# Layer 0's feed-forward by seven products over both halves of the sequence, in a two-layer block on one Trainium2 core

## The chip, the core and the metric

The kernel runs on one core of one Trainium2 chip. Its engines are TensorE (PE in the profile; PEld is its weight load), VectorE (DVE), ScalarE (ACT), GpSimd (POOL) and SyncE (SP), which issues most transfers. The metric is the device time of one execution in microseconds (us), as the median of several runs. A profile comes from one execution more; its span is what lies between the first and the last instruction.

## The reference

Two layers act on x of 1024 tokens by 1024 features, in 32-bit floats. A layer is

```python
h = rms_norm(x, g_pre_mix)
p = h @ w_in
a_pool, r_q, r_k, r_v, r_g, s_u, s_v, d_qkv, d_z, d_b, d_a = jnp.split(p, IN_SPLITS, axis=-1)
y = jnp.concatenate([pool_mixer(...), retention_mixer(...), spatial_gating_mixer(...), deltanet_mixer(...)], axis=-1)
x = x + rms_norm(y @ w_out, g_post_mix)
h = rms_norm(x, g_pre_ffn)
a, b = jnp.split(h @ w_up, 2, axis=-1)              # 2 x 2816 columns
a = causal_dwconv(a, conv_w) + conv_b               # three taps along the tokens
x = x + rms_norm((gelu(a) * b) @ w_down, g_post_ffn)
```

The four mixers are a windowed mean, a retention in chunks of 128 tokens, a gated spatial mixing, and a gated delta rule in chunks of 64 with a triangular solve per chunk. Retention, delta rule and both convolutions carry state along the tokens, so a half of the sequence needs the half before it.

## The kernel before

**Halves and precision.** The sequence is worked in two halves of 512 tokens. "Mixers (l,h)" means layer l, half h. A 32-bit operand is split into a rounded part (hi, on ScalarE) and the remainder (lo, on VectorE), and a product is three TensorE matmuls: hi·hi, hi·lo, lo·hi.

**The stages.** `win(l,h)` makes the input products (`a_unit`: one weight tile of 128 columns against 512 tokens, 24 matmuls; `b_units`: token blocks against 256 or 264 columns) and runs the mixers. `out(l,h)` is the output projection with the two norms behind it; `to_hT` transposes the normalized rows (L369) and splits them. `early(0,1)` makes some input products of mixers (0,1) in advance. `ffn(l,h)` is the plain feed-forward: for each of 22 tiles f of 128 features, two `a_unit`s, the convolution and gate, and, for every group of two f's, the down products (L1297 to L1299) into four accumulators.

**Layer 0** runs, in this order, mixers (0,0), mixers (0,1), `ffn(0,0)`, `out(0,1)`, `win(1,0)`, `ffn(0,1)`, `out(1,0)`. The feed-forward of a half gives TensorE work while the mixers of the next half take their many short dependent steps.

**Layer 1** has another form. Inside `win(1,1)` the argument `mid` starts `plain_part(1, ...)`, a generator: it does the first NPRE = 10 f's for half 0 the plain way, two at a time, with their down products (L1054 to L1056) into an accumulator that goes to DRAM (`accD`), and yields after each group of two. `run` lets it go on by NMIX = 2 groups before `out(1,1,mid)`, then closes the left part of the on-chip memory and opens pools for operand rows (`build`), then drains the generator, opens `pA0` and `pv` on the right, and makes the rest of the up products by seven products in place of eight: the normalized rows of a half, read back from DRAM (`hnD`, written by POOL at L326), are combined by four POOL additions (L1103 to L1106), transposed (L1112) and split into seven operands per half. `up_f` does the same with a tile pair of weights (four additions at L1159, seven splits at L1154 and L1155), multiplies (L1139, 84 matmuls 256 wide per half), and undoes the combination on the way out of PSUM. Its gate output goes to DRAM (`gD`) by a POOL transfer (L1213). Ten f's do so for half 1 alone (half 0 had them plainly), twelve for both halves. `down_full` then makes the down products of both halves.

**The order.** Program order gives each instruction its priority. A planner with its own costs then places the instructions of each engine one after another: at each moment the one of highest priority that it thinks ready, so that later work fills the holes it sees. `high_priority(offset=...)` moves evictions and weight casts ahead. What the planner fixes is a static order per engine and per transfer queue; on the chip an engine waits at an instruction that isn't ready, with all that stands behind it. A pool opened in the place of a closed one waits, tile by tile, for the last reader of the memory under it. `QUICK` lists the mixers whose steps are interleaved over two or three blocks of 128 tokens (`turns`); the others do one block at a time.

```python
QUICK = ((0, 0), (1, 1))
FULL = (1,)
NPRE, NMIX = 10, 2
```

`ORD1` is the order of the mixers' steps where a half other than (0,0) is in `QUICK`; its `x` calls `mid`. `FULL` lists the layers whose normalized rows are kept in `hnD`.

Of the kernel before, what the change touches and what calls it, by code (L numbers as in the profile page):

```python
# [10 lines left out]
F32R = mybir.dt.float32r  # L11
# [8 lines left out]
P = 128  # L20
# [16 lines left out]
QUICK = ((0, 0), (1, 1))  # L37
# [19 lines left out]
FULL = (1,)  # L57
NPRE, NMIX = 10, 2
# [60 lines left out]
class Net:  # L119
# [1023 lines left out]
    def up_f(self, l, f, halves, ahead=2000):  # L1143
# [14 lines left out]
        def add(o, a):  # L1158
            V.tensor_tensor(o, o, a, ALU.add)  # L1159

        with self.tc.high_priority(offset=ahead):
# [5 lines left out]
            add(b12, b22)  # L1167
# [4 lines left out]
            add(b21, b22)  # L1172
# [40 lines left out]
        nc.gpsimd.dma_start(self.gD[l][f, :, halves[0] * HALF:halves[0] * HALF + 2 * N], c)  # L1213

# [67 lines left out]
    def ffn(self, l, h, hT, mid=None):  # L1282
        self.up = UF
        nc, t, pf, st = self.nc, self.t, self.pf[l], self.state[l]
        V = nc.vector
        acc = self.acc_tiles()
        cf = st["cf"]
        def down(g0, gs):
            us = [self.unit(t["wD"][l, f], big=i == 3) for i, f in enumerate(g0)]
            for b in range(NB):  # L1290
                tb = slice(b * P, b * P + P)
                for n in range(2):
                    s = slice(n * 512, n * 512 + 512)
                    ps = self.ps()
                    for i, f in enumerate(g0):
# [3 lines left out]
                        nc.tensor.matmul(ps, lo[:, tb], us[i][0][:, s], start=False, stop=i == len(g0) - 1)  # L1299
                    with self.tc.high_priority(offset=1500):  # L1300
                        if g0[0] == 0:
# [3 lines left out]
        prev = None  # L1305
        tail = NF - GRP if l == DEPTH - 1 and h == 1 else NF
        groups = [list(range(f, min(f + GRP, NF))) for f in range(0, NF, GRP)]
        for fs in groups:
            f0 = fs[0]
            gs = []  # L1310
            for i, f in enumerate(fs):
                if i % 2 == 0:
                    cc = self.r4("c")
                pa = self.a_unit(t["wU"][l, 2 * f], hT)
                pb = self.a_unit(t["wU"][l, 2 * f + 1], hT)
                w = lambda j: pf[:, PF_CW + 3 * f + j:PF_CW + 3 * f + j + 1]
                cb = pf[:, PF_CB + f:PF_CB + f + 1]
                with self.tc.high_priority(offset=1500):
                    c = cc[:, i % 2 * HALF:i % 2 * HALF + HALF]
                    nc.scalar.activation(c, pa, AF.Identity, bias=cb, scale=w(2))  # L1320
                    if h == 0:
                        nc.scalar.copy(cf[:, f, :], pa[:, 510:512])
# [159 lines left out]
```

## Time and profile before

| what | value |
|---|---|
| time, median of 3 runs | 2557.81 us (2556.66 to 2564.56) |
| the profiled execution | 2557.59 us |
| its span | 2555.8 us |
| mean granted clock of TensorE | 0.978 |
| TensorE busy | 2435.4 us (95%) |
| VectorE busy | 1809.1 us (71%) |
| ScalarE busy | 983.0 us (38%) |
| GpSimd busy | 272.0 us (11%) |
| instructions | 38925 |

The lines of a profile are read like this. A group (`L215 PE MATMUL psg<-hT,whi 128*128 128x512 f32 x1312 | 523.4, 399 | ...`) names the line of the kernel, the engine, the operation, the tile written and the tiles read, the size and the count; behind the bar stand the busy time in us and the mean of one in ns, then the idle time of the engine just before, with what ended it. Matmuls overlap, so the mean of one is longer than the distance of two. A wait (`PE psg L1112 <- DMA hn<-hnD: 34.9, 4, 29.5`) names who waited, for whom, the sum in us, the count and the longest. In a table by stage, a stretch of the span stands first, then its length, the busy time of each engine with its count of instructions, the granted clock (1.00 is full speed), the mean busy share of the transfer engines and GB/s. All times count from the start of the span.

### The profile page before, as it was taken

What the parts mean: (1) busy time and instruction counts of PE and PEld (TensorE: products, weight loads), DVE (VectorE), ACT (ScalarE), POOL (GpSimd) and SP (SyncE); (2) the same over time, 40 slices, a digit from 0 to 9 for tenths busy, and PEclk for the clock granted to TensorE, in tenths of its full rate; (3) what the DMA queues carried; (4) which work ended last, traced back from release to release, by engine and by line L of the source; (5) the groups of instructions that cost most, each with busy time, mean ns of one, the idle gap of its engine ahead of it and who ended that gap; (6) DMA issues with size and microseconds to landing.
All of it is one profiled execution on the core that took longest, in us unless ns stands there. A gap on an engine that the chain in (4) does not pass through costs nothing.

```text
span 2555.8 us, 38925 instructions
## 1 busy us (share of the span) xinstructions
PE 2435.4 (95%) x15220; PEld 2093.1 (82%) x15220; DVE 1809.1 (71%) x3719; ACT 983.0 (38%) x1538; POOL 272.0 (11%) x389
## 2 busy tenths in 40 slices
PE   8989998999999999999999999999949799999998
PEld 7968987877788987787788898777838699999887
DVE  7895799765655898955665689976655777774747
ACT  5333452423332553332332355234432444443412
POOL 2321113000000013100000002211020200000000
PEclk9999998999999999999999999999969899999999
DMA  5233442322223552322222354222442332222723
GB/s 182 71 89 109 131 142 82 98 76 83 79 91 124 165 163 71 91 82 76 83 91 91 128 186 149 85 84 64 165 155 78 114 101 98 96 88 80 257 67 132
DMA packets 100221, 281.00 MB, mean 110 GB/s; under 512 B 30834, under 2 KB 31154, under 8 KB 99524
## 3 DMA queue, kind: packets, MB, share of 16 engines
q1 hardware_dynamic: 91428, 248.54, 30.7%
q0 software_dynamic: 8608, 29.96, 3.4%
q8 instruction: 120, 1.97, 0.3%
q14 instruction: 65, 0.53, 0.1%
HBM read 241.20 MB, written 37.26 MB: 109 GB/s over the span
## 4 chain that ended last, share of the span: by engine, by line
PE 75%; DVE 14%; DMA 4%; issue 4%; ACT 2%; POOL 1%; SPq 0%; DVEq 0%; ACTq 0%; POOLq 0%
PE psg L215 9%; PE psg L216 9%; PE psg L214 9%; PE psg L1139 7%; PE psm L1139 4%; PE psg L1297 3%; PE psg L1298 3%; PE psg L1299 3%; DVE pr L841 3%; PE psg L235 3%; PE psg L236 3%; PE psg L237 3%; DVE wlo L205 2%; PE psh L1139 2%; DVE A L843 1%
## 5 line engine op out<-in xcount | busy, mean ns | idle before, releaser
L216 PE MATMUL psg<-hT,wlo 128*128 128x512 f32 x1312 | 524.1, 401 | 0.0
L215 PE MATMUL psg<-hT,whi 128*128 128x512 f32 x1312 | 523.4, 399 | 0.2 <-DVE hT L373 0.2
L204 ACT CAST whi<-raw 128x1024 fp32r<-128x1024 f32 (+1 forms) x290 | 301.9, 1048 | 570.6 <-PE psg L215 229.0
L214 PE MATMUL psg<-hT,whi 128*128 128x512 f32 x1312 | 518.9, 396 | 0.1
L205 DVE TENSOR_TENSOR wlo<-raw,whi 128x1024 fp32r<-128x1024 f32 (+1 forms) x267 | 329.2, 1239 | 171.5 <-ACT whi L204 166.7
L214 PEld LDWEIGHTS psg<-hT,whi 128*128 128x128 f32 x1312 | 250.4, 191 | 56.5 <-ACT tmp L436 0.5
L215 PEld LDWEIGHTS psg<-hT,whi 128*128 128x128 f32 x1312 | 247.8, 189 | 57.9 <-DVE hT L373 0.8
L216 PEld LDWEIGHTS psg<-hT,wlo 128*128 128x128 f32 x1312 | 247.5, 189 | 53.7 <-issue 0.4
L1304 DVE TENSOR_TENSOR acc<-acc,psg 128x512 f32<-128x512 f32 x160 | 109.1, 686 | 72.7 <-PE psg L1299 72.1
L236 PE MATMUL psg<-wlo,hT 128*128 128x256 f32 (+1 forms) x512 | 149.9, 294 | 7.2 <-DVE wlo L205 5.7
L235 PE MATMUL psg<-whi,hT 128*128 128x256 f32 (+1 forms) x512 | 147.1, 291 | 3.2 <-ACT tmp L436 1.9
L237 PE MATMUL psg<-whi,hT 128*128 128x256 f32 (+1 forms) x512 | 149.2, 292 | 0.0
L235 PE MATMUL psg<-whi,y 128*128 128x256 f32 x512 | 142.8, 285 | 5.8 <-ACT whi L204 3.1
L1154 ACT CAST w<-wraw 128x512 fp32r<-128x512 f32 x154 | 91.4, 620 | 143.5 <-PE psg L1139 74.9
L236 PE MATMUL psg<-wlo,y 128*128 128x256 f32 x512 | 143.6, 283 | 0.8 <-DVE rv L297 0.8
L237 PE MATMUL psg<-whi,y 128*128 128x256 f32 x512 | 143.7, 284 | 0.0
L1297 PE MATMUL psg<-whi,g 128*128 128x512 f32 x352 | 140.2, 400 | 0.0
L1298 PE MATMUL psg<-wlo,g 128*128 128x512 f32 x352 | 138.8, 394 | 0.0
L1299 PE MATMUL psg<-whi,g 128*128 128x512 f32 x352 | 138.0, 392 | 0.0
L1155 DVE TENSOR_TENSOR w<-wraw,w 128x512 fp32r<-128x512 f32 x154 | 103.2, 695 | 37.4 <-ACT w L1154 37.1
L841 DVE SCALAR_TENSOR_TENSOR pr<-A 64x1 f32<-64x1 f32 (+30 forms) x124 | 110.2, 889 | 9.8 <-POOL A L837 7.5
L236 PEld LDWEIGHTS psg<-wlo,hT 128*128 128x128 f32 x512 | 99.5, 194 | 11.3 <-DVE wlo L205 6.4
(472 smaller groups left out, 5158.9 us busy)
## 6 DMA issues: line engine op xcount, KB each, us to landing
raw<-in_wU SPq DMA_DIRECT2D x108, 512.0 KB, 3.4
raw<-in_wA SPq DMA_DIRECT2D x56, 512.0 KB, 3.8
raw<-in_wD SPq DMA_DIRECT2D x54, 512.0 KB, 3.5
wraw<-in_wU SPq DMA_DIRECT2D x44, 512.0 KB, 3.4
raw<-in_wO SPq DMA_DIRECT2D x40, 512.0 KB, 3.7
raw<-in_wB SPq DMA_DIRECT2D x24, 512.0 KB, 3.7
xs<-xb SPq DMA_DIRECT2D x24, 512.0 KB, 3.3
wraw<-in_wD SPq DMA_DIRECT2D x22, 512.0 KB, 4.6
```

Of the source, the lines that this page charges most:

```text
L204: nc.scalar.copy(hi[:, :n], raw[:, :n])
L205: eng.tensor_tensor(lo[:, :n], raw[:, :n], hi[:, :n].bitcast(F32), ALU.subtract)
L214: nc.tensor.matmul(ps, a[0], b[0], start=first, stop=False)
L215: nc.tensor.matmul(ps, a[0], b[1], start=False, stop=False)
L216: nc.tensor.matmul(ps, a[1], b[0], start=False, stop=last)
L235: self.nc.tensor.matmul(ps[:, :width], h0, hi[:, s], start=k == 0, stop=False)
L236: self.nc.tensor.matmul(ps[:, :width], h0, lo[:, s], start=False, stop=False)
L237: self.nc.tensor.matmul(ps[:, :width], h1, hi[:, s], start=False, stop=k == len(hT) - 1)
L1139: self.nc.tensor.matmul(ps[:, 256 * j:256 * j + 256], b[:, x, s], self.A[h][n][y][:, k, :], start=first and k == i == j == 0, stop=k == 3 ...
L1297: nc.tensor.matmul(ps, hi[:, tb], us[i][0][:, s], start=i == 0, stop=False)
L1298: nc.tensor.matmul(ps, hi[:, tb], us[i][1][:, s], start=False, stop=False)
L1299: nc.tensor.matmul(ps, lo[:, tb], us[i][0][:, s], start=False, stop=i == len(g0) - 1)
```

## The change

Layer 0 takes the form of layer 1. `run` loops over both layers: mixers (l,1) with the plain part inside, `up_all`, and, for layer 0, a reopening of the mixers' pools, then the down products of half 0 (`down_half(0,0)`, only f 10 to 21, since the plain part's sum is loaded from `accD`), the norm, `win(1,0)`, the down products of half 1 (`down_half(0,1)`, all 22 f's), the norm and `out(1,0)`. The down products read the gate output back from `gD`, split it again and load the down weights. `ffn` is gone. `QUICK` and `FULL` change with it. In both layers one plain group (NCOVER = 1) now stands between `out(l,1)` and the building of operands for half 1; the first single-half f's are three, then half of the building for half 0, a fourth f, and the other half. In `up_f` for one half, two of the four weight additions go from VectorE to POOL.

```diff
-QUICK = ((0, 0), (1, 1))
+QUICK = ((0, 0), (0, 1), (1, 1))
-FULL = (1,)
-NPRE, NMIX = 10, 2
+FULL = (0, 1)
+NPRE, NMIX, NCOVER = 10, 2, 1
     def mix_phase(self):
+        self.layout("right")
+        self.layout("left")
         self.layout("right", ("pw", 3), ("pa", 4), ("pr", NR), ("ph", 4))
...
-        def add(o, a):
-            V.tensor_tensor(o, o, a, ALU.add)
+        def add(o, a, eng=V):
+            eng.tensor_tensor(o, o, a, ALU.add)
+
+        G = nc.gpsimd if n == 1 else V
...
-            add(b12, b22)
+            add(b12, b22, G)
...
-            add(b21, b22)
+            add(b21, b22, G)
...
+    def up_all(self, l, y, part):
+        for _ in range(NMIX):
+            next(part)
+        self.out(l, 1, y, True)
+        for _ in range(NCOVER):
+            next(part)
+        self.A = {}
+        self.layout("left", ("pu", 1), ("pA1", 1))
+        self.rows(self.pA1, 1)
+        self.build(l, 1)
+        for _ in part:
+            pass
+        self.layout("right", ("pA0", 1), ("pv", 9))
+        self.rows(self.pA0, 0)
+        for f in range(3):
+            self.up_f(l, f, (1,))
+        self.build(l, 0, (0,))
+        self.up_f(l, 3, (1,))
+        self.build(l, 0, (1,))
+        half = list(range(4, NPRE))
+        for f in range(NPRE, NF):
+            if half:
+                self.up_f(l, half.pop(0), (1,))
+            self.up_f(l, f, (0, 1))
...
-    def ffn(self, l, h, hT, mid=None):
+    def down_half(self, l, h):
+        f0 = NPRE if h == 0 else 0
+        if h == 0:
+            for b in range(NB):
+                nc.sync.dma_start(acc[b], self.accD[b * P:b * P + P])
+        for g0 in range(f0, NF, GRP):
+            fs = list(range(g0, g0 + GRP))
+            raw = self.r4("graw")
+            gs, us = [], []
+            for i, f in enumerate(fs):
+                r = raw[:, i * HALF:i * HALF + HALF]
+                nc.sync.dma_start(r, self.gD[l][f, :, h * HALF:h * HALF + HALF])
+                g = self.r4("g", F32R)
+                self.split(g[:, :HALF], g[:, HALF:], r)
+                gs.append((g[:, :HALF], g[:, HALF:]))
+                us.append(self.unit(self.t["wD"][l, f]))
...
-        y = self.win(0, 1, hT, pre)
-        for l in range(DEPTH - 1):
-            acc = self.ffn_norm(l, 0, self.ffn(l, 0, self.to_hT(acc, True)))
+        for l in range(DEPTH):
+            keep = {}
+
+            def fill(a=acc):
+                keep["g"] = self.plain_part(l, self.to_hT(a, True))
+                next(keep["g"])
+
+            y = self.win(l, 1, hT, pre, mid=fill)
+            self.up_all(l, y, keep["g"])
+            if l == DEPTH - 1:
+                break
+            self.mix_phase()
+            acc = self.ffn_norm(l, 0, self.down_half(l, 0))
             self.load_params(l + 1)
             hT = self.to_hT(acc)
-            acc = self.out(l, 1, y)
             y = self.win(l + 1, 0, hT)
-            acc = self.ffn_norm(l, 1, self.ffn(l, 1, self.to_hT(acc, True)))
+            acc = self.ffn_norm(l, 1, self.down_half(l, 1))
             hT = self.to_hT(acc)
             acc = self.out(l + 1, 0, y)
```

More of the change, by code (lines that the diff above doesn't have):

```diff
@@ L1280, in end_block @@
             nc.sync.dma_start(self.t["out"][rows, s], xb[:, s])
-    def ffn(self, l, h, hT, mid=None):
+    def down_half(self, l, h):
         self.up = UF
-        nc, t, pf, st = self.nc, self.t, self.pf[l], self.state[l]
-        V = nc.vector
+        nc, V = self.nc, self.nc.vector
         acc = self.acc_tiles()
-        cf = st["cf"]
-        def down(g0, gs):
-            us = [self.unit(t["wD"][l, f], big=i == 3) for i, f in enumerate(g0)]
+        f0 = NPRE if h == 0 else 0
[13 more added lines that the diff above has]
+                us.append(self.unit(self.t["wD"][l, f]))
             for b in range(NB):
@@ L1294, in down @@
                     ps = self.ps()
-                    for i, f in enumerate(g0):
+                    for i in range(len(fs)):
                         hi, lo = gs[i]
@@ L1304, in down @@
                             V.tensor_tensor(acc[b][:, s], acc[b][:, s], ps, ALU.add)
[L1305 to L1322, printed above, removed]
-                    V.scalar_tensor_tensor(c[:, 1:512], pa[:, 0:511], w(1), c[:, 1:512], ALU.mult, ALU.add)
-                    V.scalar_tensor_tensor(c[:, 2:512], pa[:, 0:510], w(0), c[:, 2:512], ALU.mult, ALU.add)
-                    if h == 1:
-                        V.scalar_tensor_tensor(c[:, 0:2], cf[:, f, :], w(0), c[:, 0:2], ALU.mult, ALU.add)
-                        V.scalar_tensor_tensor(c[:, 0:1], cf[:, f, 1:2], w(1), c[:, 0:1], ALU.mult, ALU.add)
-                    nc.scalar.activation(c, c, AF.Gelu_apprx_tanh)
-                    V.tensor_tensor(c, c, pb, ALU.mult)
-                    g = self.r4("g", F32R)
-                    hi, lo = g[:, :HALF], g[:, HALF:]
-                    self.split(hi, lo, c)
-                gs.append((hi, lo))
-            if prev is not None and f0 == tail:
-                fs, gs = prev[0] + fs, prev[1] + gs
-            elif prev is not None:
-                down(*prev)
-            if mid is not None and f0 == GRP * MID:
-                mid()
-                self.up = UF
-            prev = (fs, gs)
-        down(*prev)
         return acc
@@ L1362, in run @@
         acc = self.out(0, 0, y, halves=True)
[L1363 to L1365 removed]
+        for l in range(DEPTH):
[9 more added lines that the diff above has]
+            acc = self.ffn_norm(l, 0, self.down_half(l, 0))
             self.load_params(l + 1)
             hT = self.to_hT(acc)
[L1368 removed]
             y = self.win(l + 1, 0, hT)
[L1370 removed]
+            acc = self.ffn_norm(l, 1, self.down_half(l, 1))
             hT = self.to_hT(acc)
             acc = self.out(l + 1, 0, y)
[L1373 to L1400 removed]
+            pre = None
         self.down_phase()
```

30 lines of the change are left out of this document (2 added, 28 removed).

## The prediction

> **What bounds the kernel now.** I read the page's shares first, then the chain of waits, then the engines' busy time stage by stage (stages cut where the lines of a step begin and end), and last the waits inside the stages that lose time.
>
> ```profile
> PE 2435.4 (95%) x15220; PEld 2093.1 (82%) x15220; DVE 1809.1 (71%) x3719; ACT 983.0 (38%) x1538; POOL 272.0 (11%) x389
> ...
> PE 75%; DVE 14%; DMA 4%; issue 4%; ACT 2%; POOL 1%; SPq 0%; DVEq 0%; ACTq 0%; POOLq 0%
> ```
>
> TensorE is the bound: 95% busy, and 75% of the chain. So there are two prices: TensorE time that the change removes or adds, and TensorE idle time that it opens or closes. The stages, in a table whose columns are length, busy time of each engine with instruction counts, granted clock, DMA share and GB/s:
>
> ```profile
> 12.00:290.00 278.00, 268.93 (x1930) 230.28 (x1930) 217.57 (x556) 117.24 (x192) 58.98 (x78) 0.98 0.35 104
> 318.00:849.00 531.00, 524.25 (x2877) 427.70 (x2877) 366.82 (x698) 190.05 (x287) 43.73 (x68) 0.99 0.31 99
> ...
> 898.00:1042.00 144.00, 136.13 (x810) 115.62 (x809) 126.94 (x307) 61.21 (x91) 39.62 (x37) 0.98 0.37 112
> 1042.00:1297.00 255.00, 252.17 (x1479) 201.30 (x1478) 165.32 (x332) 90.32 (x134) 12.11 (x35) 0.99 0.27 83
> 1297.00:1470.00 173.00, 173.00 (x776) 141.77 (x775) 103.70 (x161) 54.24 (x68) 2.16 (x4) 1.00 0.33 106
> ...
> 1513.00:1805.00 292.00, 278.09 (x1854) 233.28 (x1853) 233.25 (x553) 117.16 (x193) 54.31 (x60) 0.99 0.34 103
> 1805.00:1857.00 52.00, 48.10 (x385) 47.19 (x384) 30.91 (x60) 25.96 (x40) 0.54 (x1) 0.97 0.56 190
> 1857.00:1909.00 52.00, 16.01 (x73) 13.57 (x72) 26.68 (x67) 14.93 (x25) 14.12 (x17) 0.61 0.48 165
> 1909.00:1985.00 76.00, 75.70 (x328) 61.28 (x327) 39.78 (x51) 19.79 (x28) 0.00 (x0) 1.00 0.25 83
> 1985.00:2040.00 55.00, 38.18 (x260) 33.84 (x261) 43.96 (x69) 25.39 (x48) 14.80 (x16) 0.88 0.35 116
> 2040.00:2350.00 310.00, 310.00 (x2623) 310.00 (x2622) 219.50 (x337) 136.84 (x227) 15.78 (x37) 1.00 0.27 91
> 2350.00:2370.00 20.00, 14.86 (x67) 12.09 (x65) 11.07 (x12) 8.38 (x11) 1.07 (x2) 0.83 0.50 170
> 704.00:768.00 64.00, 64.00 (x278) 52.06 (x278) 35.78 (x44) 19.93 (x28) 0.00 (x0) 1.00 0.27 87
> 2048.00:2112.00 64.00, 64.00 (x544) 64.00 (x543) 50.48 (x80) 30.88 (x53) 3.37 (x8) 1.00 0.29 98
> ```
>
> From top to bottom: mixers (0,0), that is layer 0's first half; mixers (0,1) under layer 0's first feed-forward; input products (1,0), its mixers under the second feed-forward, the rest of that; mixers (1,1) with six plain f's; output projection (1,1); operand building; four plain f's and three down groups; the first single-half products; the steady products; the entry to the last down products; then two samples, of pure 128x512 and pure 128x256 products. Layer 0 loses little: 531.0 − 524.3 = 6.8 us under its first feed-forward, 2.8 under the second. Layer 1, which already has the form that layer 0 is to get, loses 3.9 + 36.0 + 0.3 + 16.8 = 57.0 us from 1805 to 2040. The waits in its two bad stretches, 1850:1910 and then 1985:2040:
>
> ```profile
> PE psg L1112 <- DMA hn<-hnD: 31.5, 2, 29.5
> ...
> POOL hnD L326 <- ACT osu L1006: 12.9, 1, 12.9
> POOL hnD L326 <- DVE rt L287: 12.2, 1, 12.2
> ```
> ```profile
> PE psm L1112 <- POOL sb L1105: 4.5, 1, 4.5
> ...
> PE psg L1112 <- DMA hn<-hnD: 3.4, 2, 2.1
> ```
>
> The building's transposes (L1112) stand in TensorE's queue ahead of the plain f's and wait 31.5 us for rows that POOL can load only after it has stored the last two normalized blocks.
>
> **The change part by part.** *Up products of layer 0.* A 128x512 product takes 64.00/278 = 0.230 us, a 128x256 one 64.00/544 = 0.1176. A plain f costs 48 of the first per half, 11.05 us. The seven products cost 84 of the second for one half (9.88) and 168 for both (19.76 against 22.10). Ten f's go to one half (10 x 1.17 = 11.7 us) and twelve to both (12 x 2.34 = 28.1): −39.8 us. That is 10% of what is replaced, not an eighth, because two narrow products cost more than a wide one. The bounds are narrow: 310 us in the steady stretch are full.
>
> *Transposes.* Building takes 7 x 4 x 2 per half, 112 in all, and 32 for the second half's hT fall away. A row of the timeline with eight of them, and the next one:
>
> ```profile
> 1508.22 1.03 PE L369 MATMUL psh<-ident,acc 128*128 128x128 f32 x8
> 1509.01 0.36 PE L237 MATMUL psg<-whi,y 128*128 128x256 f32 x1
> ```
>
> 0.79/8 = 0.10 us each, so 80 more are +8.0 us.
>
> *One plain group ahead of building, in layer 1.* Two f's and a down group of 48 are 2 x 11.05 + 11.05 = 33.1 us, more than the 31.5 us of waiting; they leave the stretch 1909:1985. But the group brings VectorE weight casts, gates and evictions into 32 us where the norms of blocks 2 and 3 run, and POOL's load queues behind those norms. Between 0 and −36.0 I take −28. In the second stretch the third single f and the split building put some 10 us of products between load and use, but the sums still queue on POOL behind single stores of gD: between 0 and −16.8 I take −6. Together −34.
>
> *The same stage in layer 0.* It is new there and loses what layer 1's still loses: 57.0 − 34 = +23 (bounds 4 to 57).
>
> *Mixers (0,1)* go to the interleaved order, under six plain f's instead of 22. The nearest row is mixers (1,1), with 292.0 − 278.1 = 13.9 us idle against 6.8 before: +7 (0 to 14).
>
> *Entry to the down products.* mix_phase closes both stacks, so weight and gate tiles wait for the last f's operands, and SP's queue holds the accD and gD loads behind those releases. Nearest is the entry in layer 1, 20.0 − 14.9 = 5.1: +5 (0 to 20, that whole window).
>
> *The norm of layer 0's half 0* had the output projection as cover. Now its products wait for it; the accumulators of the next down group are its own tiles. Blocks 2 and 3 at 1857 were the same wait, 31.5 us, which is the upper bound; below, nothing. The first b_units start block by block, 96 narrow products or 11.4 us, and the last down group's blocks end staggered over 8 × 6 × 0.230 = 11 us: 31.5 − 11.4 − 11 leaves 9, and I take +8.
>
> *Mixers (1,0) under the down products alone.* Products in 1066:1297, from the groups by line:
>
> ```profile
> L215 PE MATMUL psg<-hT,whi 128*128 128x512 f32 x198 | 79.0, 399 | 0.0
> ...
> L1299 PE MATMUL psg<-whi,g 128*128 128x512 f32 x80 | 31.7, 396 | 0.0
> ```
>
> Three lines of 198 and three of 80 make 834 x 0.230 = 192 us of cover in 231 us. down_half(0,1) has 11 x 48 x 0.230 = 121. So up to 71 us of the chain of retention and delta rule are bare, if it keeps its pace. That pace (first and last step of four blocks, in mixers (1,0) and in mixers (1,1)):
>
> ```profile
> L974 DVE SCALAR_TENSOR_TENSOR zf<-psm,pm,zf x4: 483/483/484, 1181.0 to 1296.7; 128x256 f32<-128x256 f32 x4
> ```
> ```profile
> L974 DVE SCALAR_TENSOR_TENSOR zf<-psh,pm,zf x4: 477/483/484, 1745.4 to 1792.8; 128x256 f32<-128x256 f32 x4
> ```
>
> 115.7/3 = 38.6 us a block with products in between, 15.8 where the steps run interleaved and little is between them. 121 us last for 121/192 of 231 = 146 us and leave 85, or 2.2 blocks. At 15.8 these take 35; the mixers' own TensorE work (231 − 192 = 39 us over retention and four blocks) fills some 12 of it, and the b_units of win(1,1), ready once the new hT is, another 11. 35 − 12 − 11: +12 (0 to 71).
>
> *The rest* is taken at nothing: ScalarE is 38% busy, the extra reads of gD and hnD lie in stages with a DMA share of 0.25 to 0.37, and the two additions per single f that move to POOL relieve VectorE, weighed below.
>
> **Sum.** −39.8 + 8.0 − 34 + 23 + 7 + 5 + 8 + 12 = −10.8 us on the profiled span of 2555.8, or 2545.0; the median of the runs lies 2.0 above that span, so **2547**.
>
> **A rule that speaks against it.** VectorE's groups in 1985:2040 and, steady, in 2040:2350:
>
> ```profile
> L1155 DVE TENSOR_TENSOR w<-wraw,w 128x512 fp32r<-128x512 f32 x25 | 17.3, 728 | 3.0 <-ACT w L1154 2.8
> L1159 DVE TENSOR_TENSOR wraw<-wraw 128x512 f32<-128x512 f32 x15 | 11.7, 780 | 1.6 <-DMA wraw<-in_wU 1.5
> L1211 DVE TENSOR_TENSOR c<-c,p 128x256 f32<-128x256 f32 x2 | 1.9, 956 | 0.0
> ```
> ```profile
> L1155 DVE TENSOR_TENSOR w<-wraw,w 128x512 fp32r<-128x512 f32 x129 | 85.8, 689 | 34.4 <-ACT w L1154 34.2
> L1159 DVE TENSOR_TENSOR wraw<-wraw 128x512 f32<-128x512 f32 x73 | 50.2, 688 | 1.5 <-DMA wraw<-in_wU 0.2
> ...
> L1209 DVE SCALAR_TENSOR_TENSOR c<-a,pf,c 128x512 f32<-128x512 f32 x8 | 6.0, 746 | 0.0
> ...
> L1211 DVE TENSOR_TENSOR c<-c,p 128x256 f32<-128x256 f32 x8 | 3.4, 426 | 1.0 <-ACT c L1210 0.3
> ```
> ```profile
> L1103 POOL TENSOR_TENSOR sa<-hn 128x512 f32<-128x512 f32 x4 | 5.5, 1378 | 18.8 <-DMA hn<-hnD 15.3 <-DVE w L1155 3.5
> ```
>
> The same VectorE operations take 728, 780 and 956 ns where POOL's sums run, and 689, 688 and 426 elsewhere. The Trainium skill, "SBUF — State Buffer", in its part on the two physically separate sides, says that such a VectorE operation and a POOL operation lock one shared port pair against each other for a whole instruction. The trace agrees, by 0.04 to 0.53 us.
>
> **Rivals.** *POOL blocks VectorE.* A single f costs VectorE 7 x 0.689 + 4 x 0.688 + 5 x 0.42 + 2 x 0.746 = 11.2 us against 9.88 of products; with two additions gone 9.8, but with two POOL additions of 1.38 in its way 12.5. That is 2.6 us over TensorE on three of the four consecutive singles per layer: +16, 2563. Against it: the lock is rarely met at full length in the rows above.
>
> *The chain of mixers (1,0) runs out of cover* (the other side). Place: TensorE after the last group of down_half(0,1), ahead of output projection (1,0). At 25 us a block, since this stage keeps the serial order, 2.2 blocks are 55 − 12 = 43 bare, with no early b_units: +31 on my 12, so 2578; at the old pace 71, so 2606. It decides the sign once the bare time passes 12 + 11 = 23 us. For it: the 38.6. Against it: mixers (0,0) end within 278 us with 9.1 idle.
>
> *The hole moves instead of closing*, because the planner places the plain group elsewhere or its VectorE work delays the norms: 14 us instead of 28 in each layer, +28, 2575. For it: POOL's store waits for VectorE (L326 above).
>
> *Everything new is hidden.* Tail, gap and mixers (0,1) cost nothing (−27) and both stretches close whole in both layers (−2 x (8 + 10.8)): −64; half of it is 2515.
>
> **How the numbers follow.** Forecast 0.38 (own range 2530 to 2562), all hidden 0.17, cover gone 0.21, hole moves 0.14, POOL lock 0.10. A measurement tells 0.3%, 7.7 us, from no change. Of the forecast 0.28 lie below 2550 and 0.10 within; of the lock's 0.10, 0.08 within: faster 0.28 + 0.17 = 0.45, same 0.18, slower 0.37. The range reaches from beyond the hidden case to near the bare pace: 2505 to 2600.
>
> **What would show it.** Right: layer 0's products full as in 2040:2350; L1112's wait on hn below 5 us in both layers; under 15 us idle at the two joints of the down products; last L974 of mixers (1,0) less than 40 us after the last product of down_half(0,1). Wrong: idle TensorE ahead of output projection (1,0) over 23 us, L1112 waiting 15 us or more, or single f's spaced over 11 us.

## The result and the profile after

The changed kernel takes **2661.96 us** (median; 2658.91 to 2663.86) against 2557.23 us of the kernel before on the same chip: a ratio of 1.0407, 95% interval 1.0378 to 1.0435. The change is slower by 105 us, beyond the range of 2505 to 2600. The saving in TensorE's work came almost to the microsecond (31 us); the rest of the sum, forecast at +21 (−34 + 23 + 7 + 5 + 8 + 12), is +134.

The page of the changed kernel: busy times, and the chain that ended last by engine.

```profile
span 2658.7 us, 42237 instructions
...
PE 2450.5 (92%) x16524; PEld 2164.2 (81%) x16524; DVE 1917.1 (72%) x3889; ACT 1038.1 (39%) x1679; POOL 381.9 (14%) x505
...
PE 64%; DVE 19%; DMA 6%; issue 5%; ACT 4%; POOL 1%; SPq 0%; DVEq 0%; ACTq 0%; POOLq 0%
```

TensorE's part of the chain fell from 75 to 64%, VectorE's rose from 14 to 19%. The stages, in a table by stretch with the columns of the one before the change (length, busy time of PE, PEld, DVE, ACT and POOL with counts, granted clock, DMA share, GB/s):

```profile
318.00:579.00 261.00, 239.99 (x1604) 199.22 (x1603) 206.93 (x495) 95.87 (x159) 47.10 (x64) 0.93 0.30 96
579.00:631.00 52.00, 47.59 (x386) 45.87 (x384) 31.91 (x63) 27.94 (x45) 1.64 (x3) 1.00 0.63 205
631.00:665.00 34.00, 33.21 (x141) 26.46 (x142) 29.23 (x73) 14.88 (x24) 1.07 (x2) 1.00 0.56 186
665.00:693.00 28.00, 12.08 (x60) 9.64 (x58) 11.10 (x17) 8.98 (x15) 12.86 (x14) 0.63 0.51 188
693.00:737.00 44.00, 44.00 (x190) 35.69 (x191) 23.06 (x31) 10.34 (x16) 0.00 (x0) 1.00 0.19 65
737.00:827.00 90.00, 65.45 (x470) 60.87 (x469) 65.08 (x100) 40.41 (x76) 30.70 (x30) 0.89 0.29 104
827.00:1117.00 290.00, 289.54 (x2449) 289.34 (x2447) 196.29 (x290) 123.20 (x200) 24.59 (x44) 1.00 0.26 90
1117.00:1197.00 80.00, 73.39 (x303) 56.72 (x304) 57.82 (x88) 22.29 (x29) 2.83 (x7) 0.96 0.52 173
1197.00:1237.00 40.00, 20.74 (x111) 17.82 (x109) 32.62 (x101) 15.51 (x27) 2.41 (x1) 0.74 0.36 123
1237.00:1375.00 138.00, 133.46 (x799) 113.69 (x799) 111.92 (x239) 57.42 (x82) 44.97 (x37) 0.99 0.30 99
1375.00:1587.00 212.00, 189.07 (x1200) 151.74 (x1196) 176.16 (x404) 68.36 (x115) 15.63 (x39) 0.92 0.37 117
1587.00:1625.00 38.00, 37.77 (x319) 37.57 (x318) 11.47 (x18) 13.94 (x26) 0.60 (x1) 1.00 0.27 85
...
2006.00:2034.00 28.00, 14.05 (x61) 12.06 (x62) 12.09 (x17) 9.24 (x16) 12.63 (x14) 0.63 0.51 188
...
2077.00:2164.00 87.00, 64.70 (x456) 60.10 (x455) 63.50 (x98) 39.78 (x75) 30.81 (x30) 0.88 0.30 106
```

In order: mixers (0,1) under six plain f's, output projection (0,1), the plain group as cover, building for half 1, the rest of the plain part, the first single-half products with the second building, the steady products, the down products of half 0, its norm, input products (1,0), mixers (1,0) under the down products of half 1, output projection (1,0); at the end layer 1's building and first singles.

Note the steady row: 2449 matmuls in 290 us are 0.118 us each, the price of the forecast. Then note a row like 737:827. Its 470 matmuls, 56 of them transposes at 0.10 us and the rest nearly all 128x256 at 0.118, are worth 55 us; the stretch takes 90. Idle TensorE is 24.6 us of the missing 35 (90.00 − 65.45). The rest is *busy* time in which less than full work is done: some 6 us of it by the half clock (TensorE is busy for 12.9 us there while the granted clock is half), and the rest where a matmul stands alone, for its record lasts 0.28 us and more, against 0.118 from one to the next. So a stretch is better measured by its **loss**: its length less its matmuls at their full-speed prices (0.230 us for 512 columns, 0.118 for 256, 0.10 for 128, less for the few narrow ones). Worked out that way for the same stages of both kernels, to within some us, since the narrow matmuls have no price of their own:

| stage of layer 0 | loss before, us | loss after, us |
|---|---|---|
| mixers (0,1), with what runs under them | 26 | 40 |
| output projection (0,1) | 1 | 7 |
| cover, building, plain part, singles, steady | – | 2 + 22 + 0 + 35 + 2 |
| down products of half 0; its norm | – | 12; 27 |
| input products (1,0) | 17 | 10 |
| mixers (1,0), with what runs under them | 12 | 42 |
| output projection (1,0) | 1 | 1 |
| **sum** | **57** | **200** |

The matmuls of layer 0 from 318 us on, at their prices, fell from 1138 to 1107 us. In layer 1 the loss from output projection (1,1) to the end fell from 92 to 80 and that of mixers (1,1) rose from 27 to 30. −31 + 143 − 12 + 3 = +103, and the spans differ by 2658.7 − 2555.8 = 102.9.

Three waits of the changed kernel, from its lists of waits in 631:693, in 1197:1237 and in 737:827 (who waits for whom: us in total, times, longest):

```profile
PE psg L1114 <- DMA hn<-hnD: 9.6, 2, 7.0
```
```profile
PE psh L371 <- DVE acc L326: 11.4, 2, 8.9
...
PE psh L371 <- DVE rt L287: 6.4, 2, 4.0
```
```profile
POOL sa L1105 <- DVE c L1213: 11.3, 2, 10.0
```

The wait of 31.5 us that the cover was meant for is 9.6 here. The norm of half 0 stands bare: its transposes (L371) wait for it. And building for half 0 waits for POOL, whose first addition (L1105) needs a gate tile of type c that VectorE has yet to read (L1213); the wait of 10.0 us ends at 809 us, ahead of the store of the gate output at 812 us.

### The profile page after: what moved, and what is told of

Its sections match the earlier page's. It is cut to its first block, busy times and chain, and to the rows that moved or that the text cites. A ratio compares the mean times of both kernels' runs of the same rounds, so it can differ in the third digit from the quotient of the medians.

```text
span 2658.7 us, 42237 instructions
## 1 busy us (share of the span) xinstructions
PE 2450.5 (92%) x16524; PEld 2164.2 (81%) x16524; DVE 1917.1 (72%) x3889; ACT 1038.1 (39%) x1679; POOL 381.9 (14%) x505
## 4 chain that ended last, share of the span: by engine, by line
PE 64%; DVE 19%; DMA 6%; issue 5%; ACT 4%; POOL 1%; SPq 0%; DVEq 0%; ACTq 0%; POOLq 0%
PE psg L1141 13%; PE psm L1141 7%; PE psg L217 4%; PE psg L216 4%; PE psg L218 4%; DVE pr L843 3%; PE psh L1141 3%; DVE wlo L207 2%; PE psg L237 2%; PE psg L1337 2%; PE psg L239 2%; PE psg L238 2%; DVE A L845 2%; PE psg L1338 2%; PE psg L1339 2%
## 5 line engine op out<-in xcount | busy, mean ns | idle before, releaser
L206 ACT CAST whi<-raw 128x1024 fp32r<-128x1024 f32 (+1 forms) x230 | 239.8, 1048 | 487.9 <-PE psg L217 161.9
L207 DVE TENSOR_TENSOR wlo<-raw,whi 128x1024 fp32r<-128x1024 f32 (+1 forms) x207 | 255.1, 1235 | 123.3 <-ACT whi L206 121.7
L216 PE MATMUL psg<-hT,whi 128*128 128x512 f32 x768 | 306.8, 400 | 6.8 <-ACT whi L206 3.6
L217 PE MATMUL psg<-hT,whi 128*128 128x512 f32 x768 | 308.4, 402 | 0.0
L218 PE MATMUL psg<-hT,wlo 128*128 128x512 f32 x768 | 307.8, 402 | 0.0
L1156 ACT CAST w<-wraw 128x512 fp32r<-128x512 f32 x308 | 181.7, 619 | 278.6 <-PE psg L1141 159.8
L1157 DVE TENSOR_TENSOR w<-wraw,w 128x512 fp32r<-128x512 f32 x308 | 218.9, 733 | 78.1 <-ACT w L1156 75.6
L216 PEld LDWEIGHTS psg<-hT,whi 128*128 128x128 f32 x768 | 147.8, 192 | 42.0 <-ACT whi L206 4.9
L217 PEld LDWEIGHTS psg<-hT,whi 128*128 128x128 f32 x768 | 145.9, 190 | 32.9 <-issue 0.8
L218 PEld LDWEIGHTS psg<-hT,wlo 128*128 128x128 f32 x768 | 145.6, 190 | 32.1 <-issue 0.7
L1337 PE MATMUL psg<-whi,g 128*128 128x512 f32 x272 | 107.8, 417 | 11.7 <-ACT whi L206 5.7
L1141 PE MATMUL psh<-A12h,w 128*128 128x256 f32 x544 | 99.9, 286 | 16.1 <-ACT w L1156 15.9
L1339 PE MATMUL psg<-whi,g 128*128 128x512 f32 x272 | 108.2, 398 | 0.0
```

Of the source, the lines that this page charges most:

```text
L206: nc.scalar.copy(hi[:, :n], raw[:, :n])
L207: eng.tensor_tensor(lo[:, :n], raw[:, :n], hi[:, :n].bitcast(F32), ALU.subtract)
L216: nc.tensor.matmul(ps, a[0], b[0], start=first, stop=False)
L217: nc.tensor.matmul(ps, a[0], b[1], start=False, stop=False)
L218: nc.tensor.matmul(ps, a[1], b[0], start=False, stop=last)
L1141: self.nc.tensor.matmul(ps[:, 256 * j:256 * j + 256], b[:, x, s], self.A[h][n][y][:, k, :], start=first and k == i == j == 0, stop=k == 3 ...
```

## The experiments

To tell a moved loss from one that is gone, each run's span is cut at three places, at the ends of the last up product of layer 0 (L1141), of the last eviction of output projection (1,0) (L1020 in the changed kernel), and of the last up product of layer 1. **A** is from the start to the first cut, **B** to the second, **C** to the third, **D** to the end of the span. They are of the one profiled execution, which lies up to 9 us from the median (e12). The runs come from several rounds, in which the kernel before took 2554 to 2562 us; each ratio is to the kernel before of its own round, and differences of medians under some 9 us say little by themselves.

| kernel | A | B | C | D | median, us |
|---|---|---|---|---|---|
| before | A + B 1513.7 | | 839.9 | 202.2 | 2557.2 |
| after | 1116.5 | 508.4 | 830.1 | 203.6 | 2662.0 |
| e1 additions on VectorE | 1110.1 | 508.7 | 825.5 | 205.3 | 2649.6 |
| e2 no cover | 1124.4 | 511.9 | 839.3 | 203.4 | 2682.9 |
| e3 layer 1 alone | A + B 1511.3 | | 822.6 | 204.0 | 2540.1 |
| e4 (1,0) interleaved | 1114.5 | 509.0 | 815.0 | 202.4 | 2642.1 |
| e5 as e3, additions on VectorE | A + B 1511.3 | | 823.8 | 204.7 | 2540.2 |
| e6 more raw weights | 1113.4 | 501.9 | 827.2 | 203.6 | 2653.1 |
| e7 five gate tiles | 1108.3 | 507.7 | 820.7 | 202.3 | 2636.4 |
| e8 own accumulators | 1114.4 | 508.4 | 830.7 | 204.5 | 2659.3 |
| e10 norm later | 1115.5 | 484.0 | 822.5 | 202.4 | 2630.4 |
| e11 as e5, five gate tiles | A + B 1510.9 | | 812.3 | 203.9 | 2529.8 |
| e12 e1 + e4 + e7 | 1100.1 | 505.2 | 814.0 | 202.8 | 2632.5 |
| e13 (0,1) not interleaved | 1125.1 | 515.0 | 812.6 | 202.2 | 2659.3 |
| e14 down groups ahead | 1114.5 | 507.2 | 822.5 | 202.9 | 2650.9 |
| e15 e14 + e1 + e7 | 1099.3 | 506.3 | 819.9 | 204.5 | 2632.4 |
| e16 fewer VectorE sums | 1111.7 | 509.4 | 829.9 | 204.2 | 2658.3 |
| e17 e16 + e4 | 1114.7 | 505.5 | 814.9 | 202.3 | 2641.0 |

### Which layer costs: layer 1's part alone (e3, e5)

The kernel before, with only layer 1's cover, third single f and split building:

```diff
         self.out(l, 1, y, True)
+        next(part)
...
-        for f in range(2):
+        for f in range(3):
             self.up_f(l, f, (1,))
-        self.build(l, 0)
-        half = list(range(2, NPRE))
+        self.build(l, 0, (0,))
+        self.up_f(l, 3, (1,))
+        self.build(l, 0, (1,))
+        half = list(range(4, NPRE))
```

e3 has also the two additions on POOL (`G = nc.gpsimd if n == 1 else V`); e5 has all four on VectorE.

> The kernel before, with only the changes inside layer 1's feed-forward: plain group ahead of building, three single f's and the split building, two additions per single f on POOL. The predicted worth was -34 us: 2523. By the changed kernel's own trace, where layer 1 takes 535 us from output projection to the last up product against 545 before, it is only -10: 2547. The rival 'something before layer 1 disturbs it' allows -34 here.

> As the run before, but with all additions on VectorE. If POOL's additions cost time in the four consecutive single f's, this is 4 to 8 us faster than that run (about 2540); if they are harmless, the same (2547); if they relieve VectorE, slower by 2 to 6 us.

e3 takes 2540.1 us (ratio 0.993, interval 0.991 to 0.994), e5 2540.2 (the same interval). So layer 1's part is a gain of 18 us (0.7%, clear of the noise), half of the forecast 34, and all of the loss, some 120 us, is layer 0's new form. The POOL additions make no difference here.

### The cover (e2)

```diff
-NPRE, NMIX, NCOVER = 10, 2, 1
+NPRE, NMIX, NCOVER = 10, 2, 0
```

> The changed kernel without the plain group between output projection and operand building (NCOVER = 0). Theory 'the hole is half closed': the waits of the building's transposes grow from about 15 us to about 31 us in each layer, so 2662 + 2 x 16 to 2 x 25 = 2694 to 2712. Rival 'the hole only moved, the group is worth nothing': 2662 within 8 us.

2682.9 us (1.049, 1.047 to 1.051): 21 us more over two layers, between the two forecasts. The hole is back whole in layer 0; first the list of waits in 628:700, then the stretch 628:680:

```profile
PE psg L1114 <- DMA hn<-hnD: 32.8, 2, 30.1
```
```profile
628.00:680.00 52.00, 17.67 (x82) 14.78 (x83) 25.94 (x67) 13.80 (x25) 13.93 (x16) 0.61 0.45 162
```

Yet A grows by 8 only. Closing the hole saves 23 us of waiting for hn (32.8 to 9.6) and lets the products by seven start 14 us earlier (738 for 752 us), of which they give back 7 (they take 379 us with the cover and 372 without). Building stays slow with the cover too: 28 us at a clock of 0.63 in both layers of the changed kernel, for 6 us of priced work.

### The single-half products (e1, e6, e7)

Their gate outputs leave at 757, 769, 782 and 812 us in the changed kernel: 12 to 13 us apart, and 30 across the second building, against 9.88 of products for each. Three suspects are tried. e1, the POOL additions: `G = V`.

> The changed kernel with all four weight additions of a single-half f on VectorE again. Theory 'weight preparation': in the changed kernel single f's follow each other every 12.1 us against 9.88 us of products, because the two POOL additions (1.5 us each, and VectorE splits beside them of 1.6 instead of 0.69 us) lie in the serial chain that prepares one f's weights; without them the distance falls to 10.5 to 11.2 us, over 8 consecutive single f's some 8 to 14 us: 2662 to about 2650. Rival 'the additions are harmless, the loss lies at the mixers of layer 1, half 0': 2662, unchanged within 5 us. Second rival 'they relieve VectorE': slower, 2665 to 2675.

2649.6 us (1.036, 1.034 to 1.038), −12. VectorE's weight split in 737:827, after and then e1:

```profile
L1157 DVE TENSOR_TENSOR w<-wraw,w 128x512 fp32r<-128x512 f32 x41 | 32.0, 808 | 7.0 <-ACT w L1156 6.5
```
```profile
L1157 DVE TENSOR_TENSOR w<-wraw,w 128x512 fp32r<-128x512 f32 x44 | 31.4, 740 | 11.8 <-ACT w L1156 11.1
```

The mean of a split falls from 808 to 740 ns, and it hides two kinds: over the whole changed kernel the 33 splits that overlap a POOL addition take 1112 ns on average (up to 1894), the 275 that overlap none 687 (at most 695). The rule of the Trainium skill, "SBUF — State Buffer", in its part on the two physically separate sides, that such operations of VectorE and POOL lock one shared port pair against each other, agrees with this. Without the additions the singles leave at 757, 768, 781 and 806 us, and the products by seven take 374 us in place of 379 in layer 0, 373 in place of 378 in layer 1. So the POOL additions account for some 5 us a layer, but not for most of the spacing: 11, 13 and 26 us are still over 9.88.

e6, one raw weight buffer more (`wraw` bufs 3 to 4), and e7, one gate tile more; both pay with two of five p tiles:

```diff
-        return self.pu.tile([P, 1028], F32, tag="c", name=name, bufs=4)
+        return self.pu.tile([P, 1028], F32, tag="c", name=name, bufs=5)
...
-        return self.pu.tile([P, 512], F32, tag="p", name=name, bufs=5)
+        return self.pu.tile([P, 512], F32, tag="p", name=name, bufs=3)
```

> The changed kernel with four instead of three weight tiles in the up products (and, to make room, three instead of five small tiles for undoing the combination). Theory 'single f's are spaced 12.1 us because the next pair of weights can only be loaded when a tile of the pair before is free': spacing 10 to 11 us, 8 singles in a row gain 10 to 16 us, 2646 to 2652. Rival 'their VectorE work, 9.8 us and POOL's additions, sets the spacing': no change within 5 us. If the small tiles matter, the steady products lose their full rate (29.6 us for a single and a double f) and the run is slower.

> The changed kernel with five instead of four large tiles for rows, sums and gates (and three instead of five small ones). Theory 'the second half of building waits for the gate tiles of the fourth single f' (POOL's first sum waited 10 us for the gate, TensorE 6.5 us for that sum): 5 to 10 us per layer, 2642 to 2652. Rival 'the weights set the pace there': within 5 us of 2662. The run with four weight tiles carries the same three small tiles and serves as the comparison for them.

e6: 2653.1 (1.038, 1.036 to 1.041), −9, with an interval that overlaps the changed kernel's; its products by seven take 376 and 375 us, and the largest part, 6 us, lies in B, where nothing was edited. e7: 2636.4 (1.031, 1.029 to 1.033), −25. In e7 the products take 369 and 368 us in the two layers against 379 and 378, so about 10 us a layer go with the gate tile. Its first singles leave at 758, 770 and 785 us, no closer than before; the gain is at the second building, 22 us in place of 30, where POOL's first addition now waits for its rows alone:

```profile
807.20 1.54 POOL L1105 TENSOR_TENSOR sa<-hn 128x512 f32<-128x512 f32 x1 [0.29 <-DMA hn<-hnD]
```

What spaces the first singles by 12 to 13 us was not found. In 738:828 e7 fits 510 matmuls where the changed kernel had 470 in 737:827:

```profile
738.00:828.00 90.00, 69.95 (x510) 65.71 (x510) 68.12 (x104) 42.82 (x81) 32.18 (x31) 0.87 0.32 115
```

### The joint and mixers (1,0): one stock of cover (e8, e10, e14)

e8 gives three of the four accumulators of `down_half(0,1)` tiles of their own, so that its products need not wait for the norm of half 0.

```diff
+            acc = [(self.pe if b < 3 else self.pa).tile([P, D], F32, tag="acc", name=f"acc{b}") for b in range(NB)]
...
-            self.mix_phase()
+            self.mix_phase((("pe", 3),))
```

> The changed kernel with three accumulators of their own for down_half(0,1), so that its first groups need not wait for the tiles of down_half(0,0). Between the last down product of half 0 (1197 us) and the steady input products of win(1,0) (1237 us) TensorE does some 14.5 us of work in 40. Theory 'the norm's gap stays open because its cover has no tile to write to': 10 to 22 us faster, 2640 to 2652. Rival 'the cover's operands are not there either, or the planner puts it later': within 5 us of 2662.

2659.3 (1.040, 1.037 to 1.043): no change, and in its trace the down products of half 1 still start at 1376 us, so the planner put none of them into the gap. e10 takes the norm off the chain:

```diff
-            acc = self.ffn_norm(l, 0, self.down_half(l, 0))
+            acc = self.down_half(l, 0)
             self.load_params(l + 1)
             hT = self.to_hT(acc)
+            self.ffn_norm(l, 0, acc)
```

> The changed kernel, but in layer 0 the rows of half 0 are transposed for the input products of mixers (1,0) straight from the down products' accumulators, and the norms of that half are computed behind that (so these input products see rows that are not normalized; the number of operations is the same). Theory: the norm as an uncovered chain costs what its stretch 1197 to 1237 loses (40 us long, 13 us of priced products, so 27 us): 15 to 25 us less than 2662, that is 2637 to 2647. Rival: the stretch is long for other reasons (weights and tiles of the input products, the reopened pools), and the time stays within 5 us of 2662.

2630.4 (1.027, 1.024 to 1.031), −32, more than the forecast; 24 of it lie in B, the place of the edit, and 8 in C. The old gap and mixers (1,0) in e10:

```profile
1197.00:1237.00 40.00, 38.13 (x218) 32.79 (x217) 37.86 (x133) 22.24 (x40) 10.55 (x6) 0.96 0.49 164
...
1348.00:1562.00 214.00, 188.28 (x1199) 150.83 (x1197) 175.40 (x406) 68.26 (x117) 15.66 (x39) 0.92 0.36 115
```

The gap is full, and mixers (1,0) are as long as before (214 us for 212, 1199 matmuls for 1200). So taking the norm off the chain shortens B by about the 27 us that its stretch lost, and no other part of B grew. A version whose input products see normalized rows must fill the gap with other work. e14 has four own accumulators, with one operand buffer fewer, makes `down_half` a generator (`down_gen`) that yields after each group, and puts the first two down groups of half 1 (`NAHEAD = 2`) into the gap by program order:

```diff
             acc = self.ffn_norm(l, 0, self.down_half(l, 0))
+            acc1 = [self.pe.tile([P, D], F32, tag="acc", name=f"acc{b}") for b in range(NB)]
+            ahead = self.down_gen(l, 1, acc1)
+            for _ in range(NAHEAD):
+                next(ahead)
             self.load_params(l + 1)
             hT = self.to_hT(acc)
             y = self.win(l + 1, 0, hT)
-            acc = self.ffn_norm(l, 1, self.down_half(l, 1))
+            for _ in ahead:
+                pass
+            acc = self.ffn_norm(l, 1, acc1)
```

> The changed kernel, with the first two groups of down_half(0,1) (2 x 11 us of products) issued between the norm of half 0 and its transposes, into four accumulators of their own (one operand buffer fewer in that phase). The gap 1197 to 1237 lost 27 us; leaving the norm out of the way gave 31. Theory A, the gap is a loss of its own: it is filled and the rest keeps its pace, 20 to 27 us less than 2662, that is 2635 to 2642. Theory B, one stock of cover: the 22 us taken from mixers (1,0) come back there as bare chain, and the time stays within 6 us of 2662.

2650.9 (1.037, 1.035 to 1.039), −11, which neither forecast of the total has. But B, the place of the edit, is 507 us for 508, as theory B says; of the −11 us 2 lie in A and 8 in C. Two stretches, in the changed kernel and then in e14:

```profile
1200.00:1240.00 40.00, 23.22 (x126) 20.48 (x127) 30.55 (x100) 14.63 (x26) 0.47 (x1) 0.74 0.39 132
...
1380.00:1540.00 160.00, 152.38 (x896) 120.80 (x896) 130.42 (x259) 45.83 (x72) 9.90 (x23) 0.98 0.38 120
```
```profile
1200.00:1240.00 40.00, 33.44 (x174) 28.16 (x174) 34.78 (x96) 17.25 (x31) 2.51 (x1) 0.90 0.42 140
...
1380.00:1540.00 160.00, 137.60 (x821) 107.30 (x818) 135.60 (x299) 48.47 (x76) 10.47 (x23) 0.95 0.39 124
```

What TensorE gains at the gap (48 matmuls, 10 us) it lacks under mixers (1,0) (75 matmuls, 15 us). This is what one would see if B's length were that of a chain from the down products of half 0 through norm, transposes, input products and mixer steps: filling one bare place with its cover bares another. e10 and e14 fit this; what the missing operand buffer costs was not tried alone.

### The chain's pace (e4, e16, e17)

e4 interleaves the steps of mixers (1,0): `QUICK = ((0, 0), (0, 1), (1, 0), (1, 1))`, with an empty `x` where there is no `mid`.

> The changed kernel with the steps of mixers (1,0) interleaved as well. Theory 'the chain of mixers (1,0) is bare at the end': the four blocks there are done 28 us apart (1499 to 1582 us), in mixers (0,1), interleaved, 19 us; three distances of 9 us and a shorter retention (67 against 39 us) give 20 to 35 us: 2662 to 2627 - 2642. Rival 'TensorE is full enough there, the loss lies in the up products and at the norm': within 8 us of 2662. The prediction had put the bare tail at 12 us: 2650.

2642.1 (1.034, 1.032 to 1.036), −20, the edge of the theory's range, but not from there: B is 509 us, and 15 of the 20 lie in C. The interleaved steps finish earlier and stand bare, for the order has the down products of half 1 behind them. The last of the three lines of these products, in the changed kernel and then in e4:

```profile
L1339 PE MATMUL psg<-whi,g x176: 387/392/632, 1375.9 to 1539.4; 128*128 128x512 f32 x176
```
```profile
L1339 PE MATMUL psg<-whi,g x176: 387/392/401, 1435.4 to 1573.1; 128*128 128x512 f32 x176
```

So the shorter chain and the loss of its cover came together, and B doesn't tell what each is worth. In e4, from the input products on:

```profile
1236.00:1386.00 150.00, 142.53 (x836) 123.27 (x835) 127.08 (x259) 59.14 (x84) 28.81 (x32) 0.97 0.30 95
1386.00:1436.00 50.00, 33.65 (x432) 26.60 (x432) 33.66 (x102) 12.73 (x33) 11.89 (x22) 0.73 0.08 25
1436.00:1579.00 143.00, 139.01 (x674) 109.17 (x672) 106.77 (x198) 42.59 (x60) 7.53 (x22) 1.00 0.39 127
```

VectorE is busy 83% of 1375 to 1587 (176.16 of 212). e16 takes 53 us from it:

```diff
-                        if g0 == 0:
+                        if g0 == 0 or h == 1:
                             nc.scalar.copy(acc[b][:, s], ps)
```

> The changed kernel, but in down_half(0,1) every group's sums are copied into the accumulators by ScalarE in place of being added by VectorE (so only the last group's sum is left there; 80 additions, 53.3 us of VectorE in 1237 to 1587, go away). Theory V, VectorE's load sets the pace of mixers (1,0): the stretch from the last up product of layer 0 to the end of output projection (1,0) falls from 508 us to 455 to 485. Theory L, the latency of the dependent steps does: it stays at 500 or more, and the total within 12 us of 2662 (a new static order included).

> The same with mixers (1,0) interleaved. With VectorE loaded, interleaving left that stretch at 509. Theory V: with VectorE relieved the interleaved steps can overlap, 450 to 480. Theory L: the chain ends earlier by what interleaving saves on four blocks, but the down products then stand behind it and the stretch stays at 495 or more.

e16: 2658.3 (1.040, 1.038 to 1.043), B 509. e17: 2641.0 (1.034, 1.031 to 1.036), B 506, and the rest as in e4; its down products too start at 1436 us, so it says little about overlap. In e16, mixers (1,0):

```profile
1380.00:1540.00 160.00, 153.94 (x901) 122.58 (x899) 85.70 (x198) 93.52 (x158) 9.89 (x23) 0.96 0.41 131
```

VectorE fell from 130.42 to 85.70 us there, ScalarE rose from 45.83 to 93.52 of 160, and the time stayed. So VectorE's load doesn't set the pace of the serial steps. What is left, the latency of the dependent steps and the fixed order in which the cover stands, is argued here and not shown.

### The interleaving of mixers (0,1) (e13)

`QUICK = ((0, 0), (1, 1))`, and for (0,1) a serial order that starts the plain f's at the same step.

> The changed kernel, but mixers (0,1) do one block of tokens at a time as before, with the plain f's starting at the same step. Theory: with only six plain f's in place of 22 beside them these mixers are a bare chain and the interleaving shortens it, so the stage 318 to 579 gets 10 to 30 us longer: 2672 to 2692. Rival: the stage's 40 us over its priced products come from the interleaved order itself, and the time falls by 5 to 20 us.

2659.3 (1.039, 1.036 to 1.042), no change in total, which neither forecast has. The stage and its output projection:

```profile
318.00:606.00 288.00, 257.64 (x1688) 214.52 (x1686) 213.11 (x490) 103.24 (x166) 42.53 (x66) 0.91 0.30 94
606.00:647.00 41.00, 38.49 (x317) 37.37 (x315) 26.38 (x55) 23.52 (x39) 0.54 (x1) 0.99 0.67 218
```

They end at 647 us in place of 631, with 16 us more: the interleaving is worth that in its stage. The products by seven give back 7 of it (372 us for 379), as in e2. A grows by 9, B by 7, and C, where nothing was edited, falls by 17.

### Together (e11, e12, e15)

> The kernel before with layer 1's part of the change alone (one plain group ahead of building, three single f's and the split building, additions on VectorE) and with five gate tiles of type c in place of four (three p in place of five). Theory: the singles of a stage are held by the gate tiles, which gave 25 us over both layers of the changed kernel, so one layer gives 9 to 13 us on the 2540 that the same kernel with four tiles took: 2527 to 2531. Rival: most of those 25 us came from another static order or from layer 0 alone: 2536 to 2544.

> The changed kernel with the three repairs that each gained alone: all four weight additions on VectorE (-12), five gate tiles c (-25), mixers (1,0) interleaved (-20). Theory: layer 0's new form costs more in stretches that these don't touch (norm gap, entry, bare mixers, building) than its products save, so even their sum leaves it slower than 2557: 2605 if they add up, 2605 to 2625 since the first two mend the same stretch. Rival: the singles and the bare mixers were the whole loss, and it comes to 2560 or less.

> The same with five gate tiles c and all weight additions on VectorE. By stretches (singles 27 in place of 35 in each layer, additions -12 at most): 16 to 28 us less than the run of e14_ahead beside it. In either case over 2600, so that the seven products in layer 0 stay slower than the 2557 of before.

e12 takes 2632.5 (1.028, 1.025 to 1.032) and e15 2632.4 (1.029, 1.027 to 1.032); both stay far slower than before, and e12 lies above its forecast of 2605 to 2625. The single gains of e12 don't add up: −30, where −12, −25 and −20 make −57. By parts, A does (−16 from −6, −8 and −2), C doesn't (−16 from −5, −9 and −15): e4's part of it was no repair of C. e15 is 18 us under e14, 15 of them in A. **e11**, the kernel before with layer 1's part and five gate tiles, takes **2529.8 us** (0.988, 0.985 to 0.991), as forecast, and beats both kernels, the one before by 1.2%. Its covered building and its singles:

```profile
1857.00:1913.00 56.00, 44.17 (x198) 35.46 (x198) 39.36 (x83) 22.26 (x37) 13.91 (x17) 0.88 0.58 202
1957.00:2037.00 80.00, 61.76 (x454) 56.94 (x454) 66.62 (x108) 38.22 (x75) 16.97 (x20) 0.91 0.34 112
```

The hole of before (16.01 us busy in the 52 from 1857, clock 0.61) is now mostly work, and C is 812 us for 840.

## Why the prediction was wrong

*Up products and transposes, −39.8 + 8.0.* Right: layer 0's matmuls at their prices fell by 31.

*One plain group ahead of building, −34 taken in layer 1.* Right in mechanism, half in size: 18 us (e3, e5). In the changed kernel's layer 1 the hole shrank from a loss of 43 (with building) to 21, and the stretch of singles didn't gain at all: 26 before, 34 after. The 31.5 us of waiting that the group was to fill were not the whole of the hole: building itself is 28 us long with the cover in front of it.

*The same stage in layer 0, +23 with bounds of 4 to 57.* **This is the step that failed first**: it loses 68 us (7 + 2 + 22 + 35 + 2; 67 over output projection (0,1) before). Its base of 57.0 us was TensorE's idle time, which counts as work all of a matmul at half clock or standing alone; by length less priced matmuls the same stretch of layer 1 before lost 7 + 43 + 0 + 26 = 76, and of the 19 us between the two some 12 are the half clock. And the repair of 34 taken off it was too large: with the measured 18 the term would have been 58.

*Mixers (0,1), +7 (0 to 14).* 14, the upper bound. *Entry to the down products, +5 (0 to 20).* 12, inside the bounds.

*The norm of half 0, +8 (0 to 31.5).* 27, and 24 in B when it is off the chain (e10). The working let the first narrow products and the staggered end of the last down group hide 22 us of it. Narrow products did run in the 40 us (75 of the 96), but those of a block only behind its norm, and 27 us were lost beside them: VectorE works on the four norms until 1235 us (32.62 us busy in 1197:1237), and the transposes wait for it (11.4 + 6.4 us, above).

*Mixers (1,0), +12 (0 to 71).* The stage loses 42 us where it lost 12, so +30, and the input products lose 7 less. The term priced the bare blocks at 15.8 us each, the pace of interleaved steps, though these mixers keep the serial order. The four blocks end 27.8 us apart, near the 25 of the second rival:

```profile
L976 DVE SCALAR_TENSOR_TENSOR zf<-psm,pm,zf x4: 477/478/479, 1498.8 to 1582.2; 128x256 f32<-128x256 f32 x4
```

The tail runs from the last product of `down_half(0,1)` to output projection (1,0):

```profile
1540.00:1587.00 47.00, 33.47 (x292) 28.61 (x288) 40.81 (x142) 20.40 (x41) 5.74 (x16) 0.71 0.33 112
```

It has 33.47 us busy at a clock of 0.71, and its loss is 24; the other 18 of the 42 are lost while down products still run.

With the measured terms the sum is −31 − 12 + 67 + 14 + 12 + 27 − 7 + 30 + 3 = +103. None of the five losses was taken above the middle of its bounds, and the range reached only as far as one rival; the upper bounds together would have allowed some +160. All five came out higher than taken. A common cause is argued and not shown: in the old form `ffn` lay as cover beside every chain of layer 0, while in the new one most of its products run alone in the steady stretch, where they need no chain beside them. No run put products by seven beside the mixers of layer 0. The 35 us of the singles are not of this kind.

*The rivals.* POOL blocks VectorE: 12 us over the whole kernel (e1), near the 16 of this rival, but nothing in e3 against e5; the sign that was set for it, singles over 11 us apart, came true, and stays so without POOL's additions. Cover of mixers (1,0) gone: it fits the pace of the blocks, but is one loss of several. The hole moves: in part (9.6 us of waiting in layer 0 and 8.6 in layer 1, for the marks of 5 and 15), and without any cover it costs some 10 us a layer (e2), not 28. All hidden: wrong.

*A missed rule.* The Trainium skill, "TensorE: Matmul & The Clock Gate", Part 1, says that TensorE falls to half its clock after a window of some microseconds without work and needs as long to come back, and that idle gaps over about 3 us should be avoided. The trace agrees in kind: the granted clock in it is either full or half, and the three stretches of layer 0 with the largest share of idle time have a mean of 0.63, 0.74 and 0.71. Its remark that the ramp costs under 1% of a typical kernel's span doesn't hold for this kernel: in the stages of layer 0 above TensorE is busy for 95 us while its clock is half, which costs up to 47 us, 1.8% of the span; over the whole changed kernel it is up to 76 us, 2.8%, and over the kernel before up to 36 us, 1.4%. Weighed against 1857:1909 (clock 0.61) the rule would have shown that idle time is not the whole of such a price.

**What stays open.** What spaces the single f's; whether building would keep its full clock if its waits were gone (within its 28 us TensorE stands idle for 7.0 us until rows arrive, and for 2.8, 2.6 and 2.5 us until rows and sums do); how much of mixers (1,0)'s loss is the latency of their steps and how much the order, since only VectorE's load was excluded; and what e14 would give with its operand buffer kept.

## What to carry to other kernels

Price a stretch by its length less its instructions at their full-speed durations, not by idle time: the second misses what runs slowly or singly between gaps (35 against 25 us in one stretch here). Products that lie beside dependent chains can be worth their own time plus the chain's; before such work is made cheaper in another place, add up the chains that lose their cover, and let their bounds add up in the range as well. And read an experiment by stretches, for part of its total may come from a place that wasn't edited.

## What was not expected of the hardware

Not of the chip but of the order: layer 1's code behind output projection (1,0) is the same in the changed kernel, e4, e8, e10, e13, e14, e16 and e17, and yet C differs. By their traces the planner gave TensorE three orders there. Counting a run of matmuls of one line and tile as one row, the changed kernel, e8 and e16 have the same 4214 rows in the same order, and C takes 830, 831 and 830 us. e10 and e14 share 4202 of some 4216 with each other and 4007 and 4012 with the changed kernel; C takes 823 us in both. e4, e13 and e17 share 4228 or more of some 4231 with e4 and 3758 or 3759 with the changed kernel; C takes 815, 813 and 815 us. So kernels with one order agree within 3 us, whatever was edited elsewhere, and the three orders differ by some 17 us, 0.6% of the time, in untouched code. This points to the order as the cause; it was not changed by itself.

Of the chip: short work between gaps stays slow. Building's 60 matmuls, worth 6 us, take 28 with 12.08 counted as busy (14.05 in layer 1), at a clock of 0.63 in both layers alike. The granted clock is half from 668 to 681 us, full for 3.4 us, and half again from 685 to 691 us; four transposes take 0.60 us at the full clock and 1.06 to 1.12 us at half.
